# Conv weights in 0.5 MB chunks behind given x tiles, GpSimd scaling of x tiles 1 to 7, and an earlier last x tile

## The chip, the cores and the metric

The kernel runs on one Trainium2 chip, as the same program on 8 cores, each with its own part of the data. The metric is the device time of the slowest core, in microseconds (us). Lower is better. The kernel had been tuned already: TensorE was busy 97% of the time.

An execution can fall into a slower state, in which the cores of one die (cores 0 to 3, or 4 to 7) show a lower granted clock.

## The reference

One layer of a decoder, with two token mixers side by side. Only the first lines matter here: every row of `x` is normed, and the normed rows meet a wide weight matrix.

```python
h = rmsnorm(x, g_pre_mix)
p = h @ w_in                       # columns: xv | B | C | u | gate_conv | gate_pool
A  = (B * causal_dwconv3(C * xv)) @ w_out_conv       # gated short convolution
Bp = pool_scale * group_linear(trailing_mean(u) - u) # pooling over 2, 4, 8, 16 tokens
x  = x + rmsnorm((sigmoid(gate_conv) * A + sigmoid(gate_pool) * Bp) @ w_o)
x  = x + rmsnorm(relu(rmsnorm(x) @ w_up)**2 @ w_down)
```

Each core holds 2176 tokens, which are 17 x tiles of 128 tokens by 1024 channels (0.5 MB each). `D_MODEL` is 1024.

## The kernel before

Three facts are enough to follow the argument.

- An x tile goes through a chain of four engines before a weight can meet it: load, square and square root on ScalarE, reciprocal and scaling on VectorE, transposes on TensorE, eviction of the transposes on VectorE.
- In these traces every engine runs its instructions in program order.
- The conv weights come in 24 chunks for the first half of the tokens: `j` = 0 to 7, three per `j` (columns of `xv`, `C` and `B`). A chunk is read as 0.5 MB of f32, and converted to bf16 on the way. The loads of weights are issued by GpSimd, those of x by SyncE.

```python
def x_norm(i):
    x = XS[i % 11]
    ss = stat()
    P.act(XN[i % 3], x, AF.Square, accum_out=ss, name="sq")       # ScalarE
    rstd_from(ss)                              # sqrt on ScalarE, reciprocal on VectorE
    P.ts("dve", XN[i % 3], x, ss, None, ALU.mult, name="xn")      # scaling, VectorE

def x_tr(i):                                   # 8 transposes, one eviction on VectorE
    to_hT(XN[i % 3], i, C_GM)

def a_ew(j, tg, banks):                        # the convolution's elementwise chain
    ...
    P.copy("act", v(xv), v(PS[:, bxv, :]), name="xv")
    P.tt("dve", zsl(2, 2 + nn), v(PS[:, bcg, :]), v(xv), ALU.mult, name="z")
    P.act(v(tcv), zsl(0, nn), AF.Identity, scale=cs(C_WC + j), name="cv0")
    P.stt("dve", ..., name="cv1")
    P.stt("dve", ..., name="cv2")
    P.tt("dve", dst, v(PS[:, bbg, :]), v(tcv), ALU.mult, name="Ap")
```

The head works through the first 1024 tokens (x tiles 0 to 7). `a_mm(j, tg, ...)` is the matmul of weight columns `j` with 512-token group `tg`.

```python
def head():                                    # warm-up, tiles 0 to 3, a_mm(0, 0)
    ...
    x_norm(0)
    for i in range(3):
        x_norm(i + 1)
        x_tr(i)
    ...
def head2():
    a_mm(1, 0, bk); x_norm(4); a_ew(1, 0, bk)
def head3():
    a_mm(2, 0, bk); x_norm(5); x_tr(4); x_tr(5); a_ew(2, 0, bk); x_norm(6)
def head4():                                   # second 512 tokens, 128 at a time
    x_norm(7)
    for s in range(4):
        for j in range(2):
            a_mm(j, 1, bk[j], (s * 128, s * 128 + 128))
        if s < 2:
            x_tr(6 + s)
    ...
```

After the head, ten units (`j` = 3 to 7, two groups each) also norm and transpose tiles 8 to 16 on the side. The last transpose falls into the first unit of the pool stage.

```python
for n_ in range(9):
    x_at[n_ + 1] = (8 + n_,)     # unit n_+1 norms tile 8+n_; the unit after transposes it
...
steps[n0]["f"] = lambda: (b0_first(), f0(), x_tr(16))   # first unit of the pool stage
```

The loads: tiles 0 to 3 first, then the nine chunks of `j` = 0 to 2, with tiles 4 to 10 behind the second `j`, and whole weights (three chunks in one load) of `j` = 3 to 7 as soon as there is room.

```python
for i in range(4):
    load_x(i)
for s, st in enumerate(steps):
    for _, key in W.at.get(s, ()):
        issue(key, [xload[0]] if key == ("a", 0, 0, 0) else ())
        if key == ("a", 0, 1, 2):
            for i in range(4, 11):
                load_x(i, [wl[("a", 0, 1, 0)]] if i == 4 else ())
        ...
    st["f"]()
```

Of the kernel before, what the change touches and what calls it, by code (L numbers as in the profile page):

```python
# [8 lines left out]
ALU = mybir.AluOpType  # L9
# [288 lines left out]
def build_program():  # L298
    nc = bass.Bass("TRN2", target_bir_lowering=False)
    P = Prog(nc)  # L300
# [37 lines left out]
    with stack:  # L338
# [12 lines left out]
        def arv(off, dt, shape):  # L351
            return _view(AR, off, dt, shape)
# [56 lines left out]
        steps = []  # L409
        loads = {}  # L410

        def step(w, fn):
            steps.append({"w": w, "f": fn})
# [8 lines left out]
        XN = [arv(O_T + 17696 + i * 2048, BF16, [D]) for i in range(3)]  # L422
# [23 lines left out]
        def chunk(key, c):  # L446
            base = O_W + (W.window[key] + c) * 2048
            return arv(base, BF16, [KC, 128])
# [6 lines left out]
        xload = {}  # L455

        def load_x(i, deps=()):
            xload[i] = P.dma("sp", XS[i % 11], xsrc(i), "x%d" % (i % 11), name="xload", deps=deps)
# [30 lines left out]
                 name="evacT")  # L489
            touch(b)  # L490

        def x_norm(i):
            x = XS[i % 11]
            ss = stat()
            P.act(XN[i % 3], x, AF.Square, accum_out=ss, name="sq")
            rstd_from(ss)
            P.ts("dve", XN[i % 3], x, ss, None, ALU.mult, name="xn")

        def x_tr(i):
            to_hT(XN[i % 3], i, C_GM)  # L500


        for h in range(2):
            for j in range(8):
                if h == 0 and j < 3:
                    for c in range(3):
                        loads[("a", h, j, c)] = dict(n=1)
                else:
                    loads[("a", h, j)] = dict(n=3)

        def a_keys(h, j):
            return [("a", h, j, c) for c in range(3)] if h == 0 and j < 3 else [("a", h, j)]

        def a_mm(j, tg, banks, cols=None, cset=(0, 1, 2)):
            h = 0 if tg < 2 else 1
            c0, n, kind = TGS[tg]
            lo, hi = cols or (0, n)
            for c in cset:
                wt = chunk(("a", 0, j, c), 0) if h == 0 and j < 3 else chunk(("a", h, j), c)
                for k in range(KC):  # L520
                    P.mm(PS[:, banks[c], lo:hi], wt[:, k, :], hT[:, k, c0 + lo:c0 + hi], start=(k == 0), stop=(k == KC - 1))

        def a_ew(j, tg, banks):
            bxv, bcg, bbg = banks
            h = 0 if tg < 2 else 1
            c0, n, kind = TGS[tg]
            l0 = c0 - HBASE[h]
            si = rot("cv", 2)
            xv, tcv = XV[si], TCV[si]
            if kind == "p":  # L530
                zb = ZX if (h, j) == (0, 2) else Z[j % 2]
                zsl = lambda a, b: zb[:, l0 + a:l0 + b]
                nn = n
                v = lambda ap: ap[:, 0:n]
                dst = ApT[:, j, l0:l0 + n]
                if tg == 2:
                    P.copy("act", zb[:, 0:2], ZO[:, j, :])
            else:
                zb = ZSX[rot("sx", 2)]
                zsl = lambda a, b: zb[:, :, a:b]  # L540
                nn = 8
                v = lambda ap: ap[:, 0:n].rearrange("p (s t) -> p s t", t=8)
                dst = ApT[:, j, l0:l0 + n].rearrange("p (s t) -> p s t", t=8)
                P.copy("act", zb[:, :, 0:2], SCT[:, j, :].rearrange("p (s t) -> p s t", t=2))
# [3 lines that stand above are left out]
            P.stt("dve", v(tcv), zsl(1, 1 + nn), cs(C_WC + 8 + j), v(tcv), ALU.mult, ALU.add, name="cv1")  # L548
            P.stt("dve", v(tcv), zsl(2, 2 + nn), cs(C_WC + 16 + j), v(tcv), ALU.mult, ALU.add, name="cv2")
            P.tt("dve", dst, v(PS[:, bbg, :]), v(tcv), ALU.mult, name="Ap")  # L550
            for b in banks:
                touch(b)
            if kind == "s":
                P.copy("act", SCT[:, j, :].rearrange("p (s t) -> p s t", t=2), zb[:, :, 8:10])
            elif tg in (1, 3):
                P.copy("act", ZO[:, j, :], zb[:, 1024:1026])
# [19 lines left out]
        def head():  # L576
            for z in Z + [ZX]:
                P.memset("dve", z[:, 0:2], 0.0)
            warm(22)
            x_norm(0)  # L580
            for i in range(3):
                x_norm(i + 1)
                x_tr(i)
            bk = (bank(), bank(), bank())
            a_mm(0, 0, bk, (0, 128), (0,))
            a_mm(0, 0, bk, (128, 256), (0,))
            a_mm(0, 0, bk, (256, 384), (0,))
            a_mm(0, 0, bk, (0, 128), (1,))
            x_tr(3)
            a_mm(0, 0, bk, (128, 256), (1,))  # L590
            a_mm(0, 0, bk, (256, 384), (1,))
            for s in range(4):
                a_mm(0, 0, bk, (s * 128, s * 128 + 128), (2,) if s < 3 else (0, 1, 2))
            a_ew(0, 0, bk)
        step(a_keys(0, 0), head)

        def head2():
            bk = (bank(), bank(), bank())
            a_mm(1, 0, bk)
            x_norm(4)  # L600
            a_ew(1, 0, bk)
        step(a_keys(0, 1), head2)

        def head3():
            bk = (bank(), bank(), bank())
            a_mm(2, 0, bk)
            x_norm(5)
            x_tr(4)
            x_tr(5)
            a_ew(2, 0, bk)  # L610
            x_norm(6)
        step(a_keys(0, 2), head3)

        def head4():
            x_norm(7)
            bk = [(bank(), bank(), bank()) for _ in range(2)]
            for s in range(4):
                for j in range(2):
# [4 lines that stand above are left out]
                a_ew(j, 1, bk[j])  # L623
# [3 lines left out]
        order = [(j, tg) for j in range(3, 8) for tg in (0, 1)]  # L627
        x_at = {}
        for n_ in range(9):
            x_at[n_ + 1] = (8 + n_,)  # L630
        for n_, (j, tg) in enumerate(order):
            pre, post = [], []
            for i in x_at.get(n_, ()):
                pre.append(lambda i=i: x_norm(i))
                if i + 3 < NT:
                    pre.append(lambda i=i: load_x(i + 3))
            for i in x_at.get(n_ - 1, ()):
                post.append(lambda i=i: x_tr(i))
            if n_ == 0:
                post.append(late_setup)  # L640
            a_unit(j, tg, pre, post)


        for h in range(2):
            for g in range(4):
                loads[("u", h, g)] = dict(n=2)
            for m in range(8):
                loads[("m", h, m)] = dict(n=3)
        prev_uc = {}

        def u_unit(j, tg):
# [142 lines left out]
        def b0_first():  # L794
            P.dma("sp", SPT[:, :, :], st_pool, "stp", name="stload")
            P.dma("sp", GPM, bcast(g_post_mix), "gpm")
            for i in range(3):
                load_xr(i)
        n0 = len(steps)
        phase_b(0)  # L800
        f0 = steps[n0]["f"]
        steps[n0]["f"] = lambda: (b0_first(), f0(), x_tr(16))


        for j in range(8):
# [131 lines left out]
        for h in range(2):  # L937
# [4 lines left out]
                srcs[("dn", h, j)] = w_down[j]  # L942
            for g in range(4):
                srcs[("u", h, g)] = w_u[g]
        for j in range(3):
            for c in range(3):
                srcs[("a", 0, j, c)] = w_a[j][:, c:c + 1, :]
        for nh in range(2):
            srcs[("o", nh)] = w_o[nh]
        wl = {}  # L950

        def issue(key, deps=()):
            n, c = loads[key]["n"], W.window[key]
            src = srcs[key]
            dst = arv(O_W + c * 2048, BF16, [n, 1024]) if len(src.shape) == 3 else arv(O_W + c * 2048, BF16, [n * 1024])
            wl[key] = P.dma("pool", dst, src, "w%d_%d" % (c, n), name="wload", deps=deps)

        for i in range(4):
            load_x(i)
        for s, st in enumerate(steps):  # L960
            for _, key in W.at.get(s, ()):
                issue(key, [xload[0]] if key == ("a", 0, 0, 0) else ())
                if key == ("a", 0, 1, 2):
                    for i in range(4, 11):
                        load_x(i, [wl[("a", 0, 1, 0)]] if i == 4 else ())
                if key == ("a", 0, 7):
                    P.dma("pool", WPG[:, :, :, :], w_pg, "wpg")
            st["f"]()

# [53 lines left out]
```

## Time and profile before

| | before |
|---|---|
| time | 1014.15 us, median of 3 runs (1013.36 to 1014.31) |
| spans of the 8 cores in the profiled run | 1006.8 to 1013.2 us; core 1 is the slowest |
| transposes of tiles 4 to 7 begin (core 1) | 33.2, 38.1, 45.5, 50.8 us |
| x tile 7 has landed | 47.96 us |
| first matmul with the pool weights | 138.1 us |

These are two lines of the page of the kernel before: the busy time of each engine with its share of the span, and the chain of work that ended last, by engine.

```profile
PE 987.9 (97%) x5470; PEld 486.9 (48%) x5470; DVE 481.2 (47%) x811; ACT 327.3 (32%) x661; POOL 82.2 (8%) x104
...
PE 91%; DMA 4%; DVE 2%; issue 1%; ACT 1%; POOL 0%; SPq 0%; DVEq 0%; ACTq 0%; POOLq 0%
```

TensorE (PE) is the bottleneck, so only the places in which it is not fed can give anything. The next lines are from TensorE's timeline of the kernel before: start, duration, engine, source line, operation, and in brackets the idle time just before with what ended it. Line 142 is a tile's transposes; these are tiles 4 to 7 and tile 16.

```profile
33.17 0.61 PE L142 MATMUL PS<-IDB,AR 128*128 128x128 bf16 x8
38.13 1.01 PE L142 MATMUL PS<-IDB,AR 128*128 128x128 bf16 x8 [4.35 <-DVE AR L163]
45.54 0.61 PE L142 MATMUL PS<-IDB,AR 128*128 128x128 bf16 x8 [1.09 <-DVE AR L163]
50.84 0.98 PE L142 MATMUL PS<-IDB,AR 128*128 128x128 bf16 x8 [2.02 <-DVE AR L163]
...
125.62 0.69 PE L142 MATMUL PS<-IDB,AR 128*128 128x128 bf16 x8 [4.14 <-DVE AR L163]
```

TensorE waits four times, each time for a scaling (line 163) on VectorE. For the first three the scaling is only the last link. The chain of waits from 28 to 56 us, summed by line, and the load of x tile 7 (issued at 21.63 us; the last column is the time from issue to landing) show what was behind it. (A piece that began before 28 us is counted whole, so the shares add up to more than 100%.)

```profile
by line: DMA AR<-x_p 94.0%; PE PS L138 14.5%; DVE AR L158 4.4%; ACT AR L155 4.1%; issue 3.6%; ACT STAT L155 1.1%; DVE STAT L403 0.6%; DVE AR L163 0.2%; DVEq L223 0.1%; ACTq L223 0.1%
```

```profile
AR<-x_p SPq DMA_DIRECT2D x1, 512.0 KB, 26.3
```

The wait at 125.6 us has another cause. Before it, TensorE has only the 8 matmuls of a pool unit (1.9 us) after transpose 15, where a conv unit has 24 (5.3 us). VectorE's timeline just before shows a queue in which the scaling of tile 16 (124.72) comes after the last product of a unit (122.29), the eviction of tile 15's transposes (122.90) and the reciprocal:

```profile
122.29 0.69 DVE L158 TENSOR_TENSOR AR<-PS,AR 128x512 bf16<-128x512 f32 x1
122.90 1.21 DVE L158 TENSOR_TENSOR AR<-PS,CS 128x1024 bf16<-128x1024 bf16 x1
124.03 0.15 DVE L403 RECIPROCAL STAT<-STAT 128x1 f32<-128x1 f32 x1
124.72 0.75 DVE L163 TENSOR_SCALAR AR<-AR,STAT 128x1024 bf16<-128x1024 f32 x1 [0.53 <-DVE STAT L403]
```

### The profile page before, as it was taken

Reading aid. Unit: us, or ns where it says so; the run is one execution under the profiler, and the core shown is the slowest. Engines: PE = TensorE matmul, PEld = TensorE weight load, DVE = VectorE, ACT = ScalarE, POOL = GpSimd, SP = SyncE. Lnnn points to the kernel's source line nnn. Section 1 sums busy time; section 2 is a strip of 40 time slices with the busy share of each in tenths; the row PEclk is TensorE's granted clock in tenths of the full one; section 3 lists DMA queues with packets and bytes.
Section 4 is the critical chain, followed back from the end, with each engine's and each line's share of the span. In section 5 each row is a group of like instructions: output and inputs, shape, how many; then the busy total and the mean of one; then the engine's idle time right before and its main releaser. Section 6 shows DMA issues by size and latency. Waiting matters only on the chain.

```text
span 1013.2 us, 15560 instructions; the slowest of 8 cores (1006.8 to 1013.2 us)
## 1 busy us (share of the span) xinstructions
PE 987.9 (97%) x5470; PEld 486.9 (48%) x5470; DVE 481.2 (47%) x811; ACT 327.3 (32%) x661; POOL 82.2 (8%) x104
## 2 busy tenths in 40 slices
PE   7699899999999999999999999999999999999997
PEld 4464444444555554545544444444445555544443
DVE  4467766673666766778445554301115444301012
ACT  3324432222444454333254555201113333301011
POOL 4000000000000000000000000002122000002021
PEclk9899999999999999999999999999999999999999
DMA  8999934435445552223544555923089964312032
GB/s 177 218 211 211 175 86 81 73 60 98 107 102 115 132 134 49 50 55 66 128 121 108 147 116 112 183 66 125 6 202 197 183 121 84 50 35 89 37 125 83
DMA packets 25420, 114.48 MB, mean 113 GB/s; under 512 B 3200, under 2 KB 3456, under 8 KB 20992
## 3 DMA queue, kind: packets, MB, share of 16 engines
q0 software_dynamic: 11664, 65.54, 37.9%
q1 hardware_dynamic: 13392, 47.65, 13.9%
q8 instruction: 45, 0.74, 0.3%
q14 instruction: 31, 0.25, 0.1%
q10 hardware_dynamic: 288, 0.30, 0.1%
HBM read 160.01 MB, written 19.01 MB: 177 GB/s over the span
## 4 chain that ended last, share of the span: by engine, by line
PE 91%; DMA 4%; DVE 2%; issue 1%; ACT 1%; POOL 0%; SPq 0%; DVEq 0%; ACTq 0%; POOLq 0%
PE PS L138 90%; DMA AR<-x_p 3%; DVE AR L158 1%; ACT AR L155 1%; PE PS L142 1%; DMA AR<-w_a 1%; DVE AR L168 1%; POOL AR L129 0%; SPq L129 0%; DVE STAT L403 0%; DVE AR L163 0%; ACT STAT L155 0%; DVEq L223 0%; ACT L155 0%; ACTq L223 0%
## 5 line engine op out<-in xcount | busy, mean ns | idle before, releaser
L138 PE MATMUL PS<-AR 128*128 128x512 bf16 (+1 forms) x5096 | 958.7, 350 | 1.5 <-DVE AR L158 0.9
L138 PEld LDWEIGHTS PS<-AR 128*128 128x128 bf16 x5096 | 460.5, 99 | 481.9 <-issue 5.9
L155 ACT ACTIVATE AR<-PS 128x512 f32<-128x512 f32 (+3 forms) x222 | 129.7, 587 | 402.4 <-PE PS L138 383.4
L158 DVE TENSOR_TENSOR AR<-AR 128x512 bf16<-128x512 f32 (+7 forms) x264 | 171.2, 660 | 73.1 <-ACT AR L155 59.5
L403 DVE RECIPROCAL STAT<-STAT 128x1 f32<-128x1 f32 x67 | 10.7, 159 | 242.5 <-ACT STAT L155 242.0
L158 DVE TENSOR_TENSOR AR<-PS,AR 128x512 f32<-128x512 f32 (+1 forms) x122 | 73.7, 611 | 83.4 <-PE PS L138 53.5
L155 ACT ACTIVATE AR<-PS,CS 128x512 f32<-128x512 f32 (+1 forms) x80 | 48.9, 621 | 76.8 <-PE PS L138 72.4
L168 DVE SCALAR_TENSOR_TENSOR AR<-AR,CS 128x512 f32<-128x512 f32 (+1 forms) x80 | 53.7, 672 | 40.1 <-ACT AR L155 19.2
L158 DVE TENSOR_TENSOR AR<-WPG 128x512 bf16<-128x512 f32 x53 | 36.7, 692 | 53.7 <-ACT WPG L155 53.7
L155 ACT ACTIVATE AR<-AR,CS 128x512 f32<-128x512 f32 (+1 forms) x40 | 26.3, 658 | 99.9 <-DVE AR L158 99.9
L168 DVE SCALAR_TENSOR_TENSOR AR<-PS,STAT,AR 128x1024 f32<-128x1024 f32 x33 | 42.4, 1284 | 20.5 <-DMA y_p<-AR 15.2
L158 POOL TENSOR_TENSOR AR<-AR 128x1024 f32<-128x1024 f32 x16 | 37.4, 2352 | 179.4 <-DVE AR L168 96.0
L155 ACT ACTIVATE AR<-AR 128x1024 bf16<-128x1024 f32 (+1 forms) x50 | 42.2, 843 | 23.7 <-DMA AR<-x_p 16.5
L155 ACT ACTIVATE WPG<-PS 128x512 f32<-128x512 f32 x53 | 31.5, 594 | 54.7 <-PE PS L138 53.5
L158 DVE TENSOR_TENSOR AR<-PS,CS 128x1024 bf16<-128x1024 bf16 x34 | 41.4, 1217 | 2.0 <-PE PS L142 1.8
L142 PE MATMUL PS<-IDB,AR 128*128 128x128 bf16 x272 | 22.0, 227 | 16.1 <-DVE AR L163 15.1
L142 PEld LDWEIGHTS PS<-IDB,AR 128*128 128x128 bf16 x272 | 18.2, 101 | 24.7 <-issue 19.5
L168 DVE SCALAR_TENSOR_TENSOR AR<-PS,CS,AR 128x512 f32<-128x512 f32 (+1 forms) x40 | 26.5, 662 | 0.0
L129 POOL DMA_DIRECT2D AR<-w_down x16 | 8.4, 527 | 198.6 <-PE PS L138 173.7
L129 POOL DMA_DIRECT2D AR<-w_m x16 | 8.6, 536 | 196.0 <-PE PS L138 185.3
L155 ACT ACTIVATE AR<-AR,STAT 128x1024 bf16<-128x1024 f32 x17 | 19.5, 1148 | 13.1 <-DVE STAT L403 13.1
L155 ACT ACTIVATE STAT<-STAT,CS 128x1 f32<-128x1 f32 x67 | 19.7, 294 | 6.3 <-ACT AR L155 0.4
(40 smaller groups left out, 141.1 us busy)
## 6 DMA issues: line engine op xcount, KB each, us to landing
AR<-x_p SPq DMA_DIRECT2D x32, 512.0 KB, 6.8
AR<-w_up POOLq DMA_DIRECT2D x16, 1024.0 KB, 10.9
AR<-w_down POOLq DMA_DIRECT2D x16, 1024.0 KB, 10.1
AR<-w_m POOLq DMA_DIRECT2D x16, 768.0 KB, 8.5
AR<-w_a POOLq DMA_DIRECT2D x13, 768.0 KB, 10.6
x_d<-AR SPq DMA_DIRECT2D x17, 512.0 KB, 2.7
AR<-x_d SPq DMA_DIRECT2D x17, 512.0 KB, 5.6
y_p<-AR SPq DMA_DIRECT2D x16, 512.0 KB, 3.0
```

The source lines that it names most:

```text
L129: op = self.add(q, lambda e: e.dma_start(out=out, in_=in_, **kw), reads=[in_], writes=[out], name=name, dma=(semkey, cnt))
L138: return self.add("pe", lambda e: e.matmul(out, lhsT, rhs, start=start, stop=stop), reads=[lhsT, rhs], writes=[out], signal=sig, name="mm")
L142: return self.add("pe", lambda e: e.transpose(out, in_, ident), reads=[in_, ident], writes=[out], signal=signal, name="tr")
L155: return self.add("act", lambda e: e.activation(out, in_, func, **kw), reads=rd, writes=wr, name=name)
L158: return self.add(eng, lambda e: e.tensor_tensor(out, in0, in1, op), reads=[in0, in1], writes=[out], name=name)
L168: return self.add(eng, lambda e: e.scalar_tensor_tensor(out, in0, scalar, in1, op0, op1), reads=rd, writes=[out], name=name)
L403: P.add("dve", lambda e: e.reciprocal(ss, ss), reads=[ss], writes=[ss], name="rstd")
```

## The change

It has three parts.

- **Loads.** All first-half conv weights become 0.5 MB chunks. Tiles 4 to 7 are issued right behind the chunks of `j` = 2; `j` = 3 waits for x tile 5, and `j` = 4 to 7 cannot be issued before the scaling of tile 7, which stands before them on GpSimd. The intent is that x tiles no longer share the memory path with weights that are needed much later.
- **GpSimd.** The scalings of tiles 1 to 7 move from VectorE to GpSimd, and `x_norm(5)` and `x_norm(7)` move a step earlier.
- **Shift.** Tiles 8 to 16 are normed and transposed one unit earlier, so that no tile is left for the pool stage.

```diff
-        def x_norm(i):
+        def x_norm(i, eng="dve"):
...
-            P.ts("dve", XN[i % 3], x, ss, None, ALU.mult, name="xn")
+            P.ts(eng, XN[i % 3], x, ss, None, ALU.mult, name="xn")
...
-                if h == 0 and j < 3:
+                if h == 0:
                     for c in range(3):
-                        loads[("a", h, j, c)] = dict(n=1)
+                        loads[("a", h, j, c)] = dict(n=1, early=max(0, min(j - 1, 3)) if j > 2 else 0)
...                                                    # head
-                x_norm(i + 1)
+                x_norm(i + 1, "pool")
+                flush(2 if i < 2 else 9)               # issues pending weight chunks
...                                                    # head2
-            x_norm(4)
+            x_norm(4, "pool")
             a_ew(1, 0, bk)
+            x_norm(5, "pool")
...                                                    # head3
-            x_norm(5)
             x_tr(4)
             x_tr(5)
+            x_norm(6, "pool")
             a_ew(2, 0, bk)
-            x_norm(6)
+            x_norm(7, "pool")
...                                                    # head4
-            x_norm(7)
...                                                    # units after the head
-            x_at[n_ + 1] = (8 + n_,)
+            x_at[n_] = (8 + n_,)
...
-            if n_ == 0:
+            if n_ == 1:
                 post.append(late_setup)
...
-        steps[n0]["f"] = lambda: (b0_first(), f0(), x_tr(16))
+        steps[n0]["f"] = lambda: (b0_first(), f0())
...                                                    # issue of the loads
+                if key == ("a", 0, 2, 2):
+                    for i in range(4, 8):
+                        load_x(i, [wl[("a", 0, 1, 1)]] if i == 4 else ())
...
+                elif key == ("a", 0, 3, 0):
+                    deps = [xload[5]]
+                issue(key, deps)
+                if key == ("a", 0, 3, 2):
+                    for i in range(8, 11):
+                        load_x(i, [wl[("a", 0, 3, 0)]] if i == 8 else ())
```

More of the change, by code (lines that the diff above doesn't have):

```diff
@@ L511, in a_keys @@
         def a_keys(h, j):
-            return [("a", h, j, c) for c in range(3)] if h == 0 and j < 3 else [("a", h, j)]
+            return [("a", h, j, c) for c in range(3)] if h == 0 else [("a", h, j)]
         def a_mm(j, tg, banks, cols=None, cset=(0, 1, 2)):
@@ L518, in a_mm @@
             for c in cset:
-                wt = chunk(("a", 0, j, c), 0) if h == 0 and j < 3 else chunk(("a", h, j), c)
+                wt = chunk(("a", 0, j, c), 0) if h == 0 else chunk(("a", h, j), c)
                 for k in range(KC):
@@ L645, in build_program @@
             for g in range(4):
-                loads[("u", h, g)] = dict(n=2)
+                loads[("u", h, g)] = dict(n=2, early=3)
             for m in range(8):
-                loads[("m", h, m)] = dict(n=3)
+                loads[("m", h, m)] = dict(n=3, early=3)
         prev_uc = {}
@@ L944, in build_program @@
                 srcs[("u", h, g)] = w_u[g]
-        for j in range(3):
+        for j in range(8):
             for c in range(3):
@@ L959, in build_program, with flush @@
             load_x(i)
+        pending = []
+        def flush(n):
+            for key in pending[:n]:
+                issue(key)
+                if key == ("a", 0, 2, 2):
+                    for i in range(4, 8):
+                        load_x(i, [wl[("a", 0, 1, 1)]] if i == 4 else ())
+            del pending[:n]
         for s, st in enumerate(steps):
             for _, key in W.at.get(s, ()):
-                issue(key, [xload[0]] if key == ("a", 0, 0, 0) else ())
-                if key == ("a", 0, 1, 2):
-                    for i in range(4, 11):
-                        load_x(i, [wl[("a", 0, 1, 0)]] if i == 4 else ())
-                if key == ("a", 0, 7):
+                if key in [("a", 0, 1, 2), ("a", 0, 2, 0), ("a", 0, 2, 1), ("a", 0, 2, 2)]:
+                    pending.append(key)
+                    continue
+                deps = ()
+                if key == ("a", 0, 0, 0):
+                    deps = [xload[0]]
+                elif key == ("a", 0, 3, 0):
[4 more added lines that the diff above has]
+                        load_x(i, [wl[("a", 0, 3, 0)]] if i == 8 else ())
+                if key == ("a", 0, 7, 2):
                     P.dma("pool", WPG[:, :, :, :], w_pg, "wpg")
```

## The prediction

> **What bounds the kernel now.** TensorE: busy 97% of the 1013.2 us span, 91% of the chain of waits. From 140 us on it is nearly gapless (time by windows), so only the first 140 us can give anything. The slowest core (1) loses time there in two places.
>
> 1. Head, to about 57.6 us, where the last 128-column matmuls of the second 512 tokens end. The timeline shows TensorE waiting for transposes of x tiles: 4.35 us at 38.1, 1.09 at 45.5, 2.02 at 50.8, with a granted clock of 0.80 to 0.86 in these windows. The chain of waits names the x load: x tiles 4 to 7, issued at 20 to 22 us, land at 29.0, 35.2, 42.1, 48.0, about 6.3 us each. Weights of j=3 to 7, not needed before about 60 us, are issued by 16.5 us and land between (37.1, 43.5, 49.8 us). The DMAs are full (share 1.0). The Trainium skill, "DMA: Bandwidth & Descriptors", queues section, says an engine round-robins between queue rows by packet; this trace agrees: with both queues loaded, four 0.5 MB reads take 6.2 us, of which x gets one.
>
> 2. 125.6 us: TensorE waits 4.14 us for the scaling of x tile 16 on VectorE, then runs cold (0.83 clock in 120 to 130). All eight cores show 4.14 us. VectorE is the pacer behind this: from 57.2 us it never rests except for ScalarE inside the convolution chain, 4.05 us per plain unit and 6.05 us with a tile's norm and eviction, against 5.62 us on TensorE.
>
> **What the change does.** Load order becomes: x0-3, w j=0..2, x4-7; w j=3 only once tile 5 is scaled, j=4..7 after tile 7. At 21.3 us (second chunk of j=1 lands) 4 chunks and 4 tiles remain: 8 x 1.6 us, so x7 should land at about 34 to 37 instead of 48. Seven scalings move from VectorE (0.75 us) to GpSimd. No GpSimd tensor-scalar stands in this trace; its tensor-tensor of this size takes 2.35 us. The Trainium skill, "GPSIMD Engine Reference", elementwise section, gives 1.03 cycles per element for short bodies; my estimate from it is 1.0 to 1.5 us. In the first 17 us these scalings alternate with DMA issues (0.55 us each) on one in-order queue: transposes 2 and 3 come about 1 us later or equal, hidden behind weights landing at 14.7 to 18. The j=3 issues delay scaling 6 by 1.65 us.
>
> By hand: transposes 4 to 7 at about 33, 35, 39, 42 (before 33.2, 38.1, 45.5, 50.8); the second 512 tokens' chunk ends at about 48.5 to 50.5: 7 to 9 us gained.
>
> Tile 16 moves one unit up. VectorE's total work after the head is the same 73.8 us, so VectorE paces units near 6.05 us through PSUM banks and small waits of 0.2 us (about 1 us in all), but the 4.14 us gap and cold restart go: about 4.3 us gained. Everything later shifts unchanged.
>
> **Prediction.** 1014.15 - 8 - 4.3 = about 1002 us; 997.5 to 1007. Faster by over 2% (20 us) would need more than all the head's idle time: 0.02; within 2%: 0.97; slower: 0.01.
>
> **What would show it.** x7 landing before 38 us; TensorE gaps before transposes 5 to 7 below 2 us each; transpose 7 by 44 us; no gap near 115 to 125 us; first pool-weight matmul at about 125 to 126 us instead of 138.1; 875 us after it unchanged.
>
> **What would make it wrong.** GpSimd scaling of 2.5 us or more (each adds to the chain to transposes 1 to 7, since loads queue behind them); weights of j=3 to 7 late since they wait behind scaling 7; VectorE's lag reappearing as a wait for pooled tiles or banks in the pool stage, giving back most of the 4.3 us; a cold clock after gaps.

## More of the kernel before

In the groups of instructions of the first 60 us, a scaling on VectorE takes 774 ns on average (the column after the busy time):

```profile
L163 DVE TENSOR_SCALAR AR<-AR,STAT 128x1024 bf16<-128x1024 f32 x8 | 6.2, 774 | 1.1 <-DVE STAT L403 0.7
```

## The result

| | before | after | predicted |
|---|---|---|---|
| time, median | 1014.12 us (4 runs, 1013.36 to 1014.31) | 1007.87 us (4 runs, 1007.39 to 1009.43) | 1002, 997.5 to 1007 |
| spans of the 8 cores in the profile | 1006.8 to 1013.2 | 1004.8 to 1006.9 (core 4 slowest) | |
| x tile 7 landed | 47.96 | 33.6 | 34 to 37 |
| transposes 4 to 7 | 33.2, 38.1, 45.5, 50.8 | 36.9, 39.7, 45.2, 49.3 | 33, 35, 39, 42 |
| transpose 7 to first pool-weight matmul | 87.3 | 81.7 | about 83 |
| first pool-weight matmul | 138.1 | 131.0 | 125 to 126 |
| from there to the end | 875.1 | 875.9 | 875 |

The ratio of the times is 0.9942, with a 95% interval from 0.9925 to 0.9960. A ratio here is always the mean time of one kernel's fast runs over that of the kernel before in the same rounds, so it is not quite the ratio of the medians quoted. The kernel is faster by 0.6%, half of what was predicted. Two lines of the page after, as of before:

```profile
PE 979.8 (97%) x5369; PEld 484.7 (48%) x5470; DVE 475.6 (47%) x804; ACT 326.5 (32%) x661; POOL 106.6 (11%) x121
...
PE 83%; DVE 6%; issue 4%; DMA 3%; ACT 2%; POOL 1%; DVEq 0%; ACTq 0%; POOLq 0%; SPq 0%
```

GpSimd (POOL) is 24.4 us busier, and VectorE (DVE) 5.6 us less. TensorE's timeline after, for the same five tiles:

```profile
36.86 0.61 PE L142 MATMUL PS<-IDB,AR 128*128 128x128 bf16 x8
39.71 0.93 PE L142 MATMUL PS<-IDB,AR 128*128 128x128 bf16 x8 [2.24 <-POOL AR L163]
45.20 0.61 PE L142 MATMUL PS<-IDB,AR 128*128 128x128 bf16 x8 [0.58 <-POOL AR L163]
49.32 0.61 PE L142 MATMUL PS<-IDB,AR 128*128 128x128 bf16 x8 [0.83 <-POOL AR L163]
...
118.31 0.61 PE L142 MATMUL PS<-IDB,AR 128*128 128x128 bf16 x8 [0.17 <-DVE AR L163]
```

The 4.14 us wait before tile 16 is gone: 0.17 us is left. But transpose 7 comes only 1.5 us earlier on the slowest cores, and over all eight cores not at all: its mean start is 47.8 us before and 48.3 us after. In the mean of the eight cores the span shrank by 4.0 us (1009.8 to 1005.8); the rest of the slowest core's 6.3 us is a narrower spread between the cores. That part comes with the loads: before, tile 7 landed between 42.8 and 48.0 us, and its transposes began 2.8 to 2.9 us later on every core; after, it landed between 32.2 and 34.4 us, and its transposes began 14 to 16 us later. So the loads are not to blame for the late transposes. Tile 7's load (issued at 21.96 us) lands after 11.6 us instead of 26.3, and the sum of the chain of waits from 28 to 56 us now has GpSimd's scaling at its head:

```profile
AR<-x_p SPq DMA_DIRECT2D x1, 512.0 KB, 11.6
```

```profile
by line: POOL AR L163 40.8%; DMA AR<-x_p 33.7%; PE PS L138 22.0%; ACT AR L155 10.3%; issue 9.6%; PE PS L142 7.8%; ACT STAT L155 1.2%; DVE STAT L403 1.2%; ACTq L223 0.3%; POOLq L223 0.2%; DVEq L223 0.2%; DVE AR L158 0.2%
```

In the groups by form, the seven scalings on GpSimd take 2849 ns each, 3.7 times the 774 ns on VectorE:

```profile
L163 POOL TENSOR_SCALAR AR<-AR,STAT 128x1024 bf16<-128x1024 f32 x7 | 19.9, 2849 | 15.6 <-ACT AR L155 10.2 <-DVE STAT L403 3.5 <-ACT STAT L155 1.8
```

GpSimd's timeline shows the scalings of tiles 4 to 7, with the issue of the chunks of `j` = 3 between 5 and 6:

```profile
32.01 2.85 POOL L163 TENSOR_SCALAR AR<-AR,STAT 128x1024 bf16<-128x1024 f32 x1 [10.22 <-ACT AR L155]
36.62 2.85 POOL L163 TENSOR_SCALAR AR<-AR,STAT 128x1024 bf16<-128x1024 f32 x1 [1.76 <-ACT STAT L155]
39.41 1.65 POOL L129 DMA_DIRECT2D AR<-w_a  x3
42.22 2.84 POOL L163 TENSOR_SCALAR AR<-AR,STAT 128x1024 bf16<-128x1024 f32 x1 [1.17 <-DVE STAT L403]
46.33 2.85 POOL L163 TENSOR_SCALAR AR<-AR,STAT 128x1024 bf16<-128x1024 f32 x1 [1.27 <-DVE STAT L403]
```

GpSimd is idle before each of them (the brackets), also before the one behind the issues of `j` = 3, so in this program it is not short of time: each scaling starts when its reciprocal comes, and adds 2.85 us to a chain. The reciprocals come late as well. These lines of the timeline after show tile 5's reciprocal (36.17) on VectorE directly behind the last product of `a_ew(1, 0)`, and tile 7's square (43.36) on ScalarE directly behind `cv0` of `a_ew(2, 0)`, although tile 7 had landed at 33.6 us. (Tile 6's reciprocal, at 41.89 us, likewise stood behind the eviction of tile 5's transposes at 40.75; its root was done at 36.5.)

```profile
35.57 0.69 DVE L158 TENSOR_TENSOR AR<-PS,AR 128x512 bf16<-128x512 f32 x1 [0.17 <-DVE AR L168]
36.17 0.15 DVE L403 RECIPROCAL STAT<-STAT 128x1 f32<-128x1 f32 x1
...
42.73 0.72 ACT L155 ACTIVATE AR<-AR,CS 128x512 f32<-128x512 f32 x1 [5.71 <-DVE AR L158]
43.36 1.05 ACT L155 ACTIVATE AR<-AR 128x1024 bf16<-128x1024 f32 x1
```

### The profile page after: what moved, and what is told of

Its sections match the earlier page's. It is cut to its first block, busy times and chain, and to the rows that moved or that the text cites. A ratio compares the mean times of both kernels' runs of the same rounds, so it can differ in the third digit from the quotient of the medians.

```text
span 1006.9 us, 15518 instructions; the slowest of 8 cores (1004.8 to 1006.9 us)
## 1 busy us (share of the span) xinstructions
PE 979.8 (97%) x5369; PEld 484.7 (48%) x5470; DVE 475.6 (47%) x804; ACT 326.5 (32%) x661; POOL 106.6 (11%) x121
## 3 DMA queue, kind: packets, MB, share of 16 engines
q0 software_dynamic: 13104, 65.54, 39.7%
## 4 chain that ended last, share of the span: by engine, by line
PE 83%; DVE 6%; issue 4%; DMA 3%; ACT 2%; POOL 1%; DVEq 0%; ACTq 0%; POOLq 0%; SPq 0%
PE PS L138 82%; DVE AR L168 3%; DVE AR L158 2%; ACT AR L155 2%; DMA AR<-x_p 1%; POOL AR L163 1%; PE PS L142 1%; DMA AR<-w_a 1%; POOL AR L129 0%; DVEq L223 0%; DVE STAT L403 0%; DVE AR L163 0%; ACT STAT L155 0%; ACT ZO L155 0%; ACTq L223 0%
## 5 line engine op out<-in xcount | busy, mean ns | idle before, releaser
L158 DVE TENSOR_TENSOR AR<-AR 128x512 bf16<-128x512 f32 (+7 forms) x264 | 168.9, 651 | 73.5 <-ACT AR L155 59.2
L155 ACT ACTIVATE AR<-PS,CS 128x512 f32<-128x512 f32 (+1 forms) x80 | 48.9, 621 | 76.9 <-PE PS L138 69.1
L155 ACT ACTIVATE AR<-AR,CS 128x512 f32<-128x512 f32 (+1 forms) x40 | 26.3, 658 | 104.9 <-DVE AR L158 104.9
L168 DVE SCALAR_TENSOR_TENSOR AR<-PS,STAT,AR 128x1024 f32<-128x1024 f32 x33 | 42.4, 1284 | 20.8 <-DMA y_p<-AR 16.1
L155 ACT ACTIVATE WPG<-PS 128x512 f32<-128x512 f32 x53 | 31.5, 594 | 54.0 <-PE PS L138 52.8
L129 POOL DMA_DIRECT2D AR<-w_a x32 | 17.5, 568 | 83.0 <-PE PS L138 77.9
```

The source lines that it names most:

```text
L129: op = self.add(q, lambda e: e.dma_start(out=out, in_=in_, **kw), reads=[in_], writes=[out], name=name, dma=(semkey, cnt))
L155: return self.add("act", lambda e: e.activation(out, in_, func, **kw), reads=rd, writes=wr, name=name)
L158: return self.add(eng, lambda e: e.tensor_tensor(out, in0, in1, op), reads=[in0, in1], writes=[out], name=name)
L168: return self.add(eng, lambda e: e.scalar_tensor_tensor(out, in0, scalar, in1, op0, op1), reads=rd, writes=[out], name=name)
```

## The experiments

**Theory A**: GpSimd's scaling of 2.85 us, in place of the 1.0 to 1.5 us of the prediction, holds back transposes 4 to 7. **Rival B**: the program order does it, since the norms stand behind elementwise chains on ScalarE and VectorE, on whatever engine the scaling is. **Rival C**: the weights of `j` = 3 to 7 come too late. The waits of TensorE from 0 to 140 us after the change name no conv weight at all, so C fell without a run. **Rival D**, tested on the way: the head is slowed by tiles 1 to 3, whose transposes 2 and 3 come 4 us later than before (18.0 and 22.2 us instead of 13.8 and 18.0).

All twelve runs gave correct results. "tr 7" is the start of tile 7's transposes and "pool" that of the first pool-weight matmul, each on the slowest core of the profiled run. Runs e1 to e4 shared one chip, e7, e5_order_dve, e6 and e8 a second one, and the last four a third.

| run | what it is | ratio, 95% interval | median us | tr 7 | pool |
|---|---|---|---|---|---|
| (before) | | 1 | 1014.12 | 50.8 | 138.1 |
| (after) | | 0.9942 (0.9925 to 0.9960) | 1007.87 | 49.3 | 131.0 |
| e1_dve | after, scalings on VectorE | 0.9922 (0.9905 to 0.9940) | 1005.97 | 46.0 | 127.5 |
| e2_shift | before + shift | 0.9965 (0.9947 to 0.9982) | 1009.74 | 47.9 | 130.2 |
| e3_loads | before + loads | 0.9973 (0.9956 to 0.9991) | 1011.62 | 48.9 | 132.8 |
| e4_noshift | after without the shift | 0.9998 (0.9981 to 1.0014) | 1013.15 | 48.8 | 134.0 |
| e7_pool4to7 | after, tiles 1 to 3 on VectorE | 0.9942 (0.9930 to 0.9955) | 1007.59 | 49.0 | 130.5 |
| e5_order_dve | e1 with the norms reordered | 0.9890 (0.9876 to 0.9904) | 1002.09 | 44.6 | 126.6 |
| e6_order_act | e5, tiles 6 and 7 on ScalarE | 0.9918 (0.9904 to 0.9932) | 1005.54 | 47.1 | 128.7 |
| e8_order_pool | e5, scalings on GpSimd | 0.9961 (0.9948 to 0.9975) | 1009.57 | 51.0 | 132.4 |
| r_after | after, again | 0.9949 (0.9937 to 0.9962) | 1008.33 | 49.5 | 131.4 |
| e5_again | e5, again | 0.9892 (0.9874 to 0.9910) | 1002.47 | 44.0 | 126.0 |
| e9_best | e5 with two more edits | 0.9892 (0.9877 to 0.9907) | 1002.44 | 41.7 | 124.3 |
| m_forms | after + 24 GpSimd operations | one look | 1017.25 | | |

The median of e5_again is that of its two fast runs; two more fell in the slow state (1017.33 and 1033.52 us). The slowest core is not the same one in each row, and the cores differ in the head by 1 to 4 us, so the starts only show where the time lies. On the first chip the dies differ a little: the mean clock of cores 4 to 7 over the fast runs of e2, e3 and e4 is 0.987 to 0.989, that of cores 0 to 3 is 0.993 to 0.994. Where this matters below, cores 0 to 3 are given alone: the slowest of these four, averaged over the fast runs, against the same for the kernel before in the same rounds.

### e1_dve: the scalings back on VectorE

```diff
-                x_norm(i + 1, "pool")
+                x_norm(i + 1)
...                                    # and the same for x_norm(4) to x_norm(7)
```

> The changed kernel with the scalings of tiles 1 to 7 back on VectorE; load order and tile shift kept. Theory A (a GpSimd scaling takes 2.85 us where I had estimated 1.0 to 1.5, VectorE 0.75, and that ate the head's gain): transposes 1 to 3 come back to about 12, 14, 18 us, transpose 5 to about 37, transpose 7 to about 45 (49.3 in the changed kernel), time about 1003.5 us, 4 us below the changed kernel. Rival B (the order of the norms behind the convolution of weight columns 1 and 2 sets transposes 5 to 7, whatever engine scales): only transposes 1 to 3 move, transpose 7 stays at 48 to 49, time within 1 us of the changed kernel. Rival C (the held-back weights set it): no change at all.

It ran at 0.9922, faster than the changed kernel (0.9942) by 0.2%. The two intervals overlap, so the ratios alone do not settle it; on cores 0 to 3 this run gained 8.6 us on the kernel before, and the changed kernel (r_after, on another chip) 4.6. Theory A is right in sign. (With GpSimd free, the chunks of `j` = 3 to 7 are also issued earlier, from 30.5 us on; since no wait of TensorE named them after the change, this should not matter.) But transpose 5 still came at 36.8 us and transpose 7 at 46.0, not at the 35 and 42 of the prediction. TensorE's timeline of this run:

```profile
36.77 1.01 PE L142 MATMUL PS<-IDB,AR 128*128 128x128 bf16 x8 [2.98 <-DVE AR L163]
...
46.02 0.61 PE L142 MATMUL PS<-IDB,AR 128*128 128x128 bf16 x8
```

Tile 5 had landed at 30.0 us. The timeline of all engines shows ScalarE waiting 4.52 us for tile 4 to land, and then tile 5's chain: square (32.95), square root (34.18), the product of `a_ew(1, 0)` in between on VectorE (35.00), reciprocal (35.60), scaling (35.87).

```profile
28.97 1.06 ACT L155 ACTIVATE AR<-AR 128x1024 bf16<-128x1024 f32 x1 [4.52 <-DMA AR<-x_p]
...
32.95 1.04 ACT L155 ACTIVATE AR<-AR 128x1024 bf16<-128x1024 f32 x1
...
34.18 0.29 ACT L155 ACTIVATE STAT<-STAT,CS 128x1 f32<-128x1 f32 x1
...
35.00 0.69 DVE L158 TENSOR_TENSOR AR<-PS,AR 128x512 bf16<-128x512 f32 x1 [0.17 <-DVE AR L168]
...
35.60 0.15 DVE L403 RECIPROCAL STAT<-STAT 128x1 f32<-128x1 f32 x1
35.87 0.75 DVE L163 TENSOR_SCALAR AR<-AR,STAT 128x1024 bf16<-128x1024 f32 x1
```

The square began 3 us after the tile was there, behind `cv0` of the same elementwise chain, and the reciprocal more than 1 us after its root. That elementwise chain had itself stood behind tile 4's square (28.97), which waited for its load. So rival B has a share too.

### e2_shift: the shift alone

```diff
-            x_at[n_ + 1] = (8 + n_,)
+            x_at[n_] = (8 + n_,)
...
-            if n_ == 0:
+            if n_ == 1:
...
-        steps[n0]["f"] = lambda: (b0_first(), f0(), x_tr(16))
+        steps[n0]["f"] = lambda: (b0_first(), f0())
```

> The kernel before with one thing changed: tiles 8 to 16 normed one unit earlier, so tile 16 not in the pool stage (and the late setup one unit later). Theory: this alone is nearly all of the measured gain: no 4.1 us wait and no cold clock near 120 us, time about 1009 us (5 below before). Rival: VectorE paces the stage anyway and gives it back as waits for banks or pooled tiles: 1012.5 us or more.

It ran at 0.9965: the shift alone gives 0.35%, about 3.6 us of 1014. The wait before tile 16 is gone in this run too.

### e3_loads: the loads alone

This is the changed kernel with the scalings on VectorE, the norms at the places of before, and no shift.

```diff
-                x_norm(i + 1, "pool")
+                x_norm(i + 1)
...                                    # head2, head3, head4 as before
-            x_at[n_] = (8 + n_,)
+            x_at[n_ + 1] = (8 + n_,)
```

> The kernel before with the new load order alone (chunks, waits for tiles), scalings on VectorE, norms in the old places. Theory A: x tile 7 lands near 34 us instead of 48, transpose 7 comes at 44 to 46 us instead of 50.8, time about 1008 to 1010 us. Rival B (order of norms): transpose 7 at 48 or later, time above 1011 us. Rival C: weights of j=3 come late and a new wait stands at 50 to 60 us.

It ran at 0.9973. Tile 7 landed between 31.5 and 32.7 us on the cores, some 15 us earlier than before, and its transposes began at 48.9 us in place of 50.8 on the slowest cores (46.7 in place of 47.8 in the mean of the cores). So the loads did their work, and about 13 us of it met a chain that was not ready to use it.

### e4_noshift: loads and GpSimd without the shift

```diff
-            x_at[n_] = (8 + n_,)
+            x_at[n_ + 1] = (8 + n_,)
...
-        steps[n0]["f"] = lambda: (b0_first(), f0())
+        steps[n0]["f"] = lambda: (b0_first(), f0(), x_tr(16))
```

> The changed kernel without the tile shift (tile 16 in the pool stage again), so new loads and GpSimd scaling together: if the shift is worth about 5 us, time 1012 to 1013.5 us, and the 4.1 us wait is back near 118 to 124 us. If loads and GpSimd scaling carry the gain, about 1008 us.

It ran at 0.9998, the time of the kernel before. Against e3_loads of the same rounds (0.9973) that would be a cost of 0.25%, all that the loads gave. But in each of its six runs the slowest core was one of cores 4 to 7. In the profiled run their clock from 130 to 150 us was 0.86, where it was 1.00 on cores 0 to 3, and they took 877.9 to 878.2 us from the first pool-weight matmul to the end instead of 875.2 to 875.3. On cores 0 to 3 the gain on the kernel before is 2.1 us here, 2.8 in e3_loads and 3.0 in e2_shift. So there, moving the scalings to GpSimd, with the norms that go with it, took back about 0.7 us of the loads' gain; the two parts together gave 2.1 us and the shift alone 3.0, where the whole change gains 4.6 (r_after, another chip). With the norms at the same places, e1_dve against r_after puts GpSimd at about 4 us, so the moved norms must have given some 3 us back; no run has them alone. TensorE's timeline has the wait for tile 16 back:

```profile
121.53 0.61 PE L142 MATMUL PS<-IDB,AR 128*128 128x128 bf16 x8 [3.71 <-DVE AR L163]
```

### e7_pool4to7: tiles 1 to 3 on VectorE, 4 to 7 on GpSimd

```diff
             for i in range(3):
-                x_norm(i + 1, "pool")
+                x_norm(i + 1)
```

> The changed kernel with tiles 1 to 3 scaled on VectorE and tiles 4 to 7 still on GpSimd. It splits the 4 us that GpSimd costs. If the delay of the first matmuls (18.8 us against 14.7) is what counts, transposes 1 to 3 return to about 12, 14, 18 us and the time to 1004 to 1005 us, nearly that of all scalings on VectorE. If the second set counts (2.85 us each, and the j=3 issues between them), transpose 7 stays at 47 to 49 us and the time at 1006 to 1008 us.

It ran at 0.9942, as the changed kernel does. The first weight columns' `xv` copy came at 21.9 us again, as before the change (21.5; 25.9 after it), and the time gained in that way was lost again at tile 5, as TensorE's timeline shows:

```profile
39.23 1.01 PE L142 MATMUL PS<-IDB,AR 128*128 128x128 bf16 x8 [4.47 <-POOL AR L163]
...
48.96 0.61 PE L142 MATMUL PS<-IDB,AR 128*128 128x128 bf16 x8 [0.75 <-POOL AR L163]
```

Rival D falls: the delay of tiles 1 to 3 was hidden. Tiles 4 to 7 set the time.

### e5_order_dve: VectorE, and the norms reordered

```diff
             a_mm(1, 0, bk)
-            x_norm(4)
             a_ew(1, 0, bk)
-            x_norm(5)
+            x_norm(4, "dve")
...
             a_mm(2, 0, bk)
+            x_norm(5, "dve")
             x_tr(4)
+            x_norm(6, "dve")
             x_tr(5)
-            x_norm(6)
+            x_norm(7, "dve")
             a_ew(2, 0, bk)
-            x_norm(7)
```

> All scalings on VectorE as in the first experiment, and the norms reordered: the convolution of weight columns 1 goes before the norm of tile 4, the norms of tiles 5, 6, 7 go before the convolution of weight columns 2. If the program order on VectorE and ScalarE is the second limit of the head (tile 5 landed at 30.0 and was transposed at 36.8), transpose 5 comes at 34 to 35, transpose 7 at 40 to 43 (46.0 there), and the time falls by another 2 to 3.5 us to about 0.989 to 0.990 of the kernel before. If x loads or weights limit, no change (0.992).

Two things change in the order on ScalarE and VectorE. The norm of tile 6 comes before the transposes of tile 5 and their eviction, and the norm of tile 7 before `a_ew(2, 0)`. And `a_ew(1, 0)` no longer stands behind the norm of tile 4: in e1_dve its `xv` copy came at 30.41 us, after tile 4 had landed, in e5_again at 25.34, and tile 5's square came at 30.78 instead of 32.95. It ran at 0.9890 (1002.09 us) and again, on another chip, at 0.9892. This beats both kernels: against the changed one on the same chip (r_after, 0.9949) it is 0.57% or about 6 us faster (e5_again). TensorE's timeline of the second run has transposes 4 and 5 together at 34.79, 6 at 40.58 and 7 at 43.98, with waits of at most half a microsecond before them:

```profile
34.79 1.10 PE L142 MATMUL PS<-IDB,AR 128*128 128x128 bf16 x16
...
40.58 0.61 PE L142 MATMUL PS<-IDB,AR 128*128 128x128 bf16 x8 [0.48 <-DVE AR L158]
...
43.98 0.61 PE L142 MATMUL PS<-IDB,AR 128*128 128x128 bf16 x8
```

### e6_order_act: tiles 6 and 7 scaled on ScalarE

```diff
+            if eng == "act":
+                P.act(XN[i % 3], x, AF.Identity, scale=ss, name="xn")
...
-            x_norm(6, "dve")
+            x_norm(6, "act")
...
-            x_norm(7, "dve")
+            x_norm(7, "act")
```

> As the reordered one, with tiles 6 and 7 scaled on ScalarE (about 1.15 us, as it scales tiles elsewhere). If VectorE is still the busiest of the head, 0.5 to 1.5 us better than with VectorE; if ScalarE's own queue now delays the convolution, the same or worse.

This was a miss: 0.9918, slower than e5 (0.9890). Two lines of ScalarE's timeline and one of TensorE's show why. The scaling of tile 7 (39.78) is in the way of the `xv` copy of `a_ew(2, 0)` (40.84), which empties a bank that TensorE waits for:

```profile
39.78 1.15 ACT L155 ACTIVATE AR<-AR,STAT 128x1024 bf16<-128x1024 f32 x1 [0.36 <-DVE STAT L403]
40.84 0.58 ACT L155 ACTIVATE AR<-PS 128x512 f32<-128x512 f32 x1
```

```profile
41.56 0.61 PE L138 MATMUL PS<-AR 128*128 128x128 bf16 x8 [2.54 <-ACT AR L155]
```

### e8_order_pool: the new order with GpSimd

```diff
-            x_norm(4, "dve")
+            x_norm(4, "pool")
...                                    # and the same for tiles 1 to 3 and 5 to 7
```

> The reordered norms with all of tiles 1 to 7 still on GpSimd. If GpSimd's 2.85 us per tile is the limit, it gains at most 2 us on the changed kernel (transpose 7 not before 46, since four scalings and the three j=3 issues alone take 13 us after tile 4 lands at about 30): ratio 0.992 to 0.995. If order was the whole limit, it equals the reordered one on VectorE.

It ran at 0.9961, which is 0.7% slower than e5 with the very same order, and slower than the changed kernel. With `x_norm(4)` behind `a_ew(1, 0)` the scaling of tile 4 began at 35.06 us instead of 32.01, and GpSimd's 2.85 us came on top of it. From there GpSimd had no rest until 48.1 us: the issues of `j` = 3 (1.65 us) and three scalings back to back (8.63 us). So order and engine are not two terms that can be added: the new order is good with a scaling of 0.75 us and bad with one of 2.85 us.

### r_after and e5_again: both on one chip

These are the changed kernel and e5_order_dve, without edits.

> The changed kernel again, beside the two reordered ones on the same chip: 0.994 of the kernel before, as measured first.

> The reordered kernel on VectorE again (only four of its runs were undisturbed): 0.989, so 5 to 6 us below the changed kernel on the same chip.

The ratios 0.9949 and 0.9892 repeat the first ones (0.9942 and 0.9890) within their intervals.

### e9_best: two more edits on e5

```diff
+        SQJ = arv(O_SPT + 4112, BF16, [D])
...
-            P.act(XN[i % 3], x, AF.Square, accum_out=ss, name="sq")
+            P.act(SQJ if 4 <= i < 8 else XN[i % 3], x, AF.Square, accum_out=ss, name="sq")
...
-            a_mm(2, 0, bk)
+            a_mm(2, 0, bk, cset=(0, 1))
             x_norm(5, "dve")
             x_tr(4)
+            a_mm(2, 0, bk, cset=(2,))
```

> The reordered one with two waits more taken out: tile 4 is transposed before the last third of weight columns 2, and the squares of tiles 4 to 7 write to a place of their own, so ScalarE need not wait for transpose 4. If those waits are on the critical path: transposes 4 and 5 about 1.5 us earlier, the end of the head 1 to 2 us earlier, ratio 0.987. If the convolution of weight columns 2, which the eviction of tile 6 stands behind, is the limit instead: no change, 0.989.

Squares into a place of their own need not wait until a tile's transposes have read the buffer, and tile 4's transposes come before the last eight matmuls of `j` = 2. Transpose 7 came at 41.7 us, where the prediction had put it. The time is not told apart from that of e5_again: both ratios are 0.9892.

### m_forms: what costs what on GpSimd

```diff
+            for _ in range(3):
+                P.ts("pool", BO, GPM, c, None, ALU.mult)     # scalar per partition
+            for _ in range(3):
+                P.ts("pool", BO, GPM, 0.5, None, ALU.mult)   # constant
...                                        # f32 output, bf16 input, copy, tensor by tensor
```

> The changed kernel with 24 extra operations on GpSimd between 150 and 300 us, where it is idle, three of each form on 128x1024: what makes one scaling take 2.85 us. If reading the scalar from memory costs: the forms with a constant are faster, near 1 us. If writing bf16 costs: f32 output is faster. If it is GpSimd's rate per element for any such operation: all forms take 2.3 us or more. The estimate of the prediction, 1.0 to 1.5 us, holds for none, one or some of these forms.

24 operations of 128 by 1024 elements were put on GpSimd between 285 and 347 us, in a stage where the changed kernel uses it for little else. Three of the groups by form, scaling by a scalar per partition, scaling by a constant, and a plain copy with conversion:

```profile
L163 POOL TENSOR_SCALAR AR<-AR,CS 128x1024 bf16<-128x1024 f32 x3 | 8.6, 2880 | 0.4 <-POOL AR L163 0.3
...
L163 POOL TENSOR_SCALAR AR<-AR 128x1024 bf16<-128x1024 f32 x3 | 8.3, 2768 | 0.5 <-POOL AR L163 0.3 <-DVE AR L168 0.2
...
L174 POOL CAST AR<-AR 128x1024 bf16<-128x1024 f32 x3 | 3.7, 1250 | 0.3
```

The scaling costs 2.77 to 2.88 us on average whatever its scalar, and also with f32 output or bf16 input (2.77 to 2.88). Only the copy, 1.25 us, lies where my estimate put the scaling; tensor by tensor took 2.13 to 2.16 us. So none of the three explanations that the expectation offered holds.

The run also showed a cost that I had not asked for. In its one execution it took 1017.25 us, 9 us more than the changed kernel on the same chip. TensorE's waits from 150 to 450 us name VectorE for 7.1 us of it. VectorE's operations with two inputs in SBUF were slower while GpSimd worked. First these groups of VectorE in m_forms (285 to 346 us), then the same in the changed kernel (283 to 344 us):

```profile
L168 DVE SCALAR_TENSOR_TENSOR AR<-AR,CS 128x512 f32<-128x512 f32 x14 | 14.7, 1046 | 7.4 <-ACT ZO L155 3.7 <-ACT AR L155 2.9
L158 DVE TENSOR_TENSOR AR<-AR 128x1024 f32<-128x1024 f32 x3 | 6.7, 2246 | 0.5 <-DVE AR L168 0.5
```

```profile
L168 DVE SCALAR_TENSOR_TENSOR AR<-AR,CS 128x512 f32<-128x512 f32 x16 | 12.0, 751 | 8.4 <-ACT AR L155 3.9 <-ACT ZO L155 3.7
...
L158 DVE TENSOR_TENSOR AR<-AR 128x1024 f32<-128x1024 f32 x4 | 4.9, 1225 | 0.4
```

The operations that read PSUM kept their times (692, 679 and 1283 ns, against 692, 683 and 1284). In the head of the changed kernel the pairs of the first form kept their 1.61 us beside a scaling on GpSimd, so this is not what cost the time there.

## Why the prediction was right or wrong

**Right: what bounds the kernel and where.** Only the first 138 us changed. From the first pool-weight matmul on, it is 875.1 us before and 875.9 after; of the 0.8 us, 0.32 is a wait for a pooled tile at 131.7 us and 0.2 longer waits near 367 and 513 us; the rest is not placed.

**Right: the loads.** Tile 7 was predicted to land at 34 to 37 us and did at 33.6, just before that range.

**Right: the shift.** The wait of 4.14 us at tile 16 went, the waits of 0.2 us that were to replace it are there (0.17 and 0.24), and the stretch from transpose 7 to the first pool-weight matmul is 5.6 us shorter (5.1 in the mean of the cores), where 4.3 had been predicted. Not all of the 5.6 is the shift. About 1.1 us is TensorE's clock right after transpose 7: on core 1 before it was 0.93 from 50 to 75 us and the stretch took 87.3 us; on cores 0, 2, 5 and 7, at 1.00 there and like core 1 at 0.97 from 75 to 135 us, it took 86.0 to 86.2. And without the shift (e4_noshift) the stretch was already down to 85.2 or 85.3 us on seven cores, so against that run the shift is worth 3.6. Alone (e2_shift) it gives 0.35%, or 3.6 us.

**Wrong: the head.** The step that failed is "transposes 4 to 7 at about 33, 35, 39, 42 ... 7 to 9 us gained". It measured 36.9, 39.7, 45.2, 49.3, and 1.5 us on the slowest cores, with nothing in the mean of the cores. The sum then reads 1.5 + 5.6 - 0.8 = 6.3 us, in place of 8 + 4.3. Two terms of that placement were off, and they do not simply add (e8).

- The first was written in the prediction: "my estimate from it is 1.0 to 1.5 us" for a scaling on GpSimd. It took 2.85 us. Undoing it (e1_dve) gives 0.2%, or about 4 us on cores 0 to 3; with the better order it is worth 0.7% (e5 against e8). The prediction named 2.5 us or more as what would make it wrong, but gave that too little weight in its range. It had a better number at hand: the trace had a two-input GpSimd operation of this size at 2.35 us.
- The second was in no line of the prediction: its text does not say what stands before a tile's square, reciprocal and scaling in program order on ScalarE and VectorE. With a scaling even shorter than its estimate (e1_dve, 0.75 us) transposes 5 and 7 still came at 36.8 and 46.0 us. In the program these instructions stand behind the elementwise chains of `a_ew(1, 0)` and `a_ew(2, 0)`, and `a_ew(1, 0)` behind the wait for tile 4's load. With the fast scaling and the old places (e3_loads), landing 15 us earlier moved transpose 7 by 2 us. With the fast scaling and the norms reordered (e5), the kernel takes 1002.09 us, which is the 1002 that was predicted, for another program than the one in the diff.

**Wrong, but without effect.** Transposes 2 and 3 were to come "about 1 us later or equal"; they came 4 us later. e7 shows that it costs nothing. The issues of `j` = 3 were to "delay scaling 6 by 1.65 us"; GpSimd stood idle for 1.17 us between them and that scaling, which waited for its reciprocal.

**Named as a risk, and there: a cold clock.** The mean granted clock of the eight cores from 10 to 50 us, in the profiled runs, is 0.90 before, 0.88 after and 0.88 in e1_dve, but 0.95 in e5_order_dve and 0.84 in e8_order_pool. The prediction took nothing off for it. e5 and e8 ran on one chip and differ in the scaling engine alone, so a part of the 0.7% between them may be the speed of the matmuls and not the waiting itself; the runs do not separate the two.

**Named as a risk and not seen:** late weights of `j` = 3 to 7; and pool-stage waits that give back most of the 4.3 us (0.8 came back).

**Left open.** In e9_best transpose 7 comes 2 us earlier than in e5_again on the slowest cores, but 0.7 us in the mean of all eight, and the first pool-weight matmul 0.1 us in the mean; so little was gained, and what takes the rest back was not followed. Whether GpSimd's 2.85 us would be less beside an idle VectorE was not measured: VectorE worked in all these stretches.

## What to carry to other kernels

When an earlier load is to pay, follow the tile through every in-order engine up to the bottleneck: what stands before each of its instructions in program order decides, not when its data is there. Cost an operation that moves to another engine with no less than the slowest thing the trace shows of that size on that engine (2.35 us here, and it took 2.85), and run the form alone if the trace has none. And take a change of several parts apart early: here one part gave most of the gain, while another ate into what the rest gave. Look at the clock of both dies before you read such small differences: by its ratio alone, e4_noshift tells that two of the parts gave nothing.

## What the Trainium skill lacked or had wrong

- "GPSIMD Engine Reference", section "Elementwise — side-by-side cycle accounting", gives 1.03 cycles per element for bodies of at most two operations, and section "Engine selection" calls one-input work "roughly line-rate". The runs differ for a scaling of 128 by 1024 elements: 2.85 us in the head, 2.77 to 2.88 us on average in m_forms, whatever the scalar and the types, against 0.77 us on VectorE. Only a copy with conversion (1.25 us) came near it. The elementwise section's measured 2.6 cycles per element for a two-input operation was the closer guide: tensor by tensor took 2.35 us before and 2.13 to 2.16 us in m_forms, so a one-input scaling is dearer than a two-input product, which the page does not say.
- The same page, section "Specifications", says that GpSimd shares its SBUF interfaces with VectorE, with contention for VectorE operations with two SBUF inputs. m_forms agrees, and gives a size, which that page lacks: 2246 ns instead of 1225 and 1046 instead of 751 on average for such operations, and no change for those that read PSUM.
- "DMA: Bandwidth & Descriptors", section "Queues, rings and completion order", says that an engine takes turns between queue rows by packet. The trace before agrees: with weights and x both queued, 442 packets of the weights' queue and 440 of x's went through between 29 and 48 us (core 1). What the page lacks is what equal turns mean for the time: packets of the two queues differ, so the weights had 75.5% of the engines' time and x 26.7% (as the view adds them up), one x tile of 0.5 MB landed per four reads of that size, about every 6.3 us, and tile 7 landed at 48 us rather than at 34.
- No page that I read says how a chain across in-order engines is to be placed by hand: 15 us of earlier landing gave 2 us of earlier transposes (e3_loads).
